# The first layer's MLP up-projection by Strassen's seven block products

## The chip, the cores and the metric

One Trainium2 chip, one core of it. The metric is the device time of one execution in microseconds (us), the median of three runs. Inputs and outputs lie in the chip's memory; all arithmetic is in float32, and each operand of a product is split into a rounded part (hi) and a rest (lo), so that a product of two matrices is three TensorE products: hi x hi, hi x lo, lo x hi.

## The reference

Two layers over 512 latent rows and 256 context rows of width 1024. What matters here is the MLP sub-layer of the first layer, which runs over all 768 rows:

```python
def sq_relu_mlp(h, lw):
    return jnp.square(jax.nn.relu(h @ lw["w1"])) @ lw["w2"]

x = layer_norm(alpha * x + g2 * sq_relu_mlp(modulate(x, sh2, sc2), lw), ln2_g[l], ln2_b[l])
```

w1 is 1024 x 4096 and w2 is 4096 x 1024. The factors sh1, sc1, g1, sh2, sc2, g2 ("modulation vectors") of each layer are six pieces of 1024 of silu(c) @ w_ada + b_ada, one set for the latent stream and one for the context stream.

## The kernel before

The kernel is written with a framework that tracks what each instruction reads and writes, sets the waits and schedules the instructions of each engine ahead of time: an instruction is placed once its operands and its buffer are expected to be free, earlier program text first. On the chip each engine then runs its list in that order.

**The first layer's MLP** (`mlp`, from L1215). The 768 rows stand transposed in two halves of 384 tokens (`hT[0]`, `hT[1]`), hi and lo. The 4096 hidden columns go in eight groups of 512 (NGRP = 8), each in four units of 128 columns. For a group, every unit is multiplied with each half over eight K chunks: 24 products of 128x128 by 128x384, accumulated in one PSUM bank (`termsA`, `chain` at L151). The bank is read by ScalarE (relu, L1236) and VectorE (square, L1237), and the square is split to hi (ScalarE cast, L145) and lo (VectorE subtraction, L146) in `U`. Then the group's down-projection: for each half of the output columns and each of six row tiles, twelve products of 512 columns over the group's four units, added to the row sums `acc` by VectorE (L1276; by ScalarE in group 0). The last group's down-projection is in `mlp_end`, with the layer norm behind it.

**Weights.** w1 comes in loads of 512 KB on SP's queue to the tile `raw` (three buffers, shared with all other loads), and is split to tiles `wh` (ScalarE) and `wl` (VectorE), five buffers each (`unitsA`; L145, L146). w2 likewise (`unitsB`, `split`; L140, L141).

**PSUM.** Four single banks (`bank`) and two tiles of two banks (`two`) for the whole kernel.

**Modulation chunks** (`mod_chunk`, L371 on). 512 columns of a modulation vector set: eight multiply-adds per stream on VectorE (L381, L383) from four loads of 512 KB, a split, two one-row products, an addition (L392), a store. A chunk is six steps; `next(mods)` in other code takes one step, so that the chunks run beside that code. The chunks of layer 1 all run in the first layer's MLP: four of two streams, then eight of one stream. Eight chunks of layer 0 run beside the gate projections of layer 0 (`gates`); beside those of layer 1 none do.

**Other pieces of the stage.** In group 6 the gated residual is taken up (L1279 on GpSimd, L1280 on VectorE) from row tiles loaded ahead. After group 5 the first weights of layer 1 are loaded (`self.early`, `unitsB(..., ahead=True)`).

Of the kernel before, what the change touches and what calls it, by code (L numbers as in the profile page):

```python
# [10 lines left out]
F32 = mybir.dt.float32  # L11
# [22 lines left out]
def shape_tables():  # L34
    """Constants that depend on the shapes alone."""
# [45 lines left out]
    # even and odd frequencies of the latent rows' first half  # L81
# [8 lines left out]
class Act:  # L90
    """transposed rows: per part (hi, lo) the tiles [128, k1 - k0, n] with their ranges of K chunks"""
# [13 lines left out]
class Build:  # L105
    def __init__(self, tc, A):
        self.tc, self.nc, self.A = tc, tc.nc, A
        self.es = ExitStack()
        self.n = 0
        self.nsplit = 0  # L110
        self.om = {}

# [16 lines left out]
    def raw(self, pieces, shape):  # L129
        """pieces: (slice in the raw tile, view in DRAM)"""  # L130
        r = self.t(self.wp, shape, "raw", bufs=3)
        for sl, v in pieces:
            self.nc.sync.dma_start(r[sl], v)
        return r
# [17 lines left out]

    def bank(self):
        return self.t(self.ps, [128, 512], "one", bufs=4)
# [7 lines left out]
    def unitsA(self, view, c0, nchunk, K=8):  # L162
        """units of 128 output columns over all K chunks; two units from two loads of half the K chunks"""
# [10 lines left out]
    def unitsB(self, view, k0, nk, colpieces, scale=None, ahead=False):  # L174
        """per K chunk the (hi, lo) views of the given output columns, times scale; in tiles of their own if ahead"""
# [20 lines left out]

    def termsA(self, unit, act, sl=slice(None), K=8):
# [6 lines left out]
    def termsB(self, lh, units, cols=slice(None)):  # L204
        """lh(k) -> (hi, lo) views [128, 128 tokens]"""
# [6 lines left out]
    def rstd(self, ms, n):  # L212
        """(ms + eps) ** -0.5, in place"""
# [7 lines left out]
    def ln_stats(self, x, st=None):  # L221
        """(mean, rstd) columns of the rows x; st has the halves' statistics if given"""
# [17 lines left out]
    def modulate(self, x, pool, cols, act, sl, quick, sums=None):  # L240
        """layer norm of the rows x, modulated, transposed, to the columns sl of act; a generator of its stages"""
# [5 lines left out]
        else:  # L247
            # the mean from the sums, the squared deviations on the scalar engine
# [19 lines left out]
        if quick:  # L268
            # half the chunks each on the vector and the scalar engine
# [20 lines left out]
    def skew(self, starts, start, newest=False, fill=iter(()), at=0):  # L290
        """a generator for each of the starting stages; within a stage the oldest or the newest first; a step of fill per stage from the given one on"""
# [25 lines left out]
    def mod_start(self, pool):  # L317
        """shift and scale of the first layer's first sub-layer: three quarters on the tensor engine, one on the vector engine; a generator of its pieces"""
# [51 lines left out]
    def mod_chunk(self, l, q, streams, pool):  # L370
        """512 modulation columns: products and sums over K chunks on the vector engine, the sum over partitions by a ones row; a generator of its pieces"""  # L371
# [28 lines left out]
    def load_cols(self, l, sub, s):  # L400
        """scale + 1 and shift as columns"""
# [20 lines left out]
    def where(self, i):  # L422
        """half and columns of token tile i"""
# [14 lines left out]
    def fourier(self, l, pre):  # L438
        """pre: the projected rows, of each token tile or of each column half and two tiles"""
# [3 lines left out]
        with ExitStack() as es:  # L443
# [8 lines left out]
            for t in range(2):  # L452
                # sum and difference of the halves of the latent rows
# [60 lines left out]
    def small_proj(self, l, hT, es_mla, es_gqa):  # L514
# [9 lines left out]
        # four heads by all tokens, or all heads by half the tokens  # L524
# [3 lines left out]
        with ExitStack() as es:  # L528
            tp = self.pool(es, f"sp{l}")
            def rope_tables(nm, scale):  # L530
                """rotary cos and signed sin with the gain folded in"""
# [24 lines left out]
            def normT(n, gain, dst, i):  # L556
                """the rows n [128, 256] transposed, by gain, to dst [128, 2, 2, tokens]"""
# [14 lines left out]
            def rope(pool_tag, kn, nh, cos, sin, i, bufs):  # L572
                """a + b = the rotated kn [128, nh, 64]"""
# [120 lines left out]
    def gates(self, l, hT, tp):  # L694
# [4 lines left out]
        mods = self.mod_chunks(0, [(q, 2) for q in range(4, 12)], tp) if l == 0 else iter(())  # L699
# [510 lines left out]
    def mlp(self, l, hT, pre, rp, lq):  # L1210
# [15 lines left out]
        for g in range(NGRP):  # L1226
# [4 lines left out]
            def w1(j, unit, h, n0, n, ps=None):  # L1231
# [7 lines left out]
                if g:  # L1239
                    next(mods, None)  # L1240
# [301 lines left out]
```

## Time and profile before

| | |
|---|---|
| time, median of 3 runs | 2323.4 us (2322.81 to 2329.74) |
| profiled execution, span from first to last instruction | 2328.0 us |
| TensorE busy | 2251.7 us (97%), mean granted clock 0.988 |
| VectorE busy | 1469.0 us (63%) |
| ScalarE busy | 1006.4 us (43%) |
| GpSimd busy | 341.4 us (15%) |
| mean DMA rate | 123 GB/s |

The profiled execution is one run, on its own; its time beyond the span is not listed, so its span stands for it. It lies 4.6 us above the median of the runs. Busy time is the union of an engine's instructions; the products are pipelined, so the duration of one is longer than the distance to the next, and the pace is read from start to start.

### The profile page before, as it was taken

The numbers are of one execution on the slowest core, as the hardware profiler recorded it, in microseconds if no ns is written. First come the engines' busy times: TensorE is split into PE (matmuls) and PEld (weight loads), VectorE is DVE, ScalarE is ACT, GpSimd is POOL, SyncE is SP. The second block draws the span as 40 slices with busy tenths as digits, with TensorE's granted clock in tenths as the row PEclk, the third lists the DMA queues.
The fourth block names the chain that finished last, engine by engine and source line by source line (L and its number), as shares of the span: only waits on it lengthen the run. The fifth ranks groups of instructions, "written<-read, shape, count | busy, mean of one in ns | idle before, by whom it ended". The sixth has DMA issues, their size and how long they took to land. (4 is left out here: it accounts for less than half of the span.)

```text
span 2328.0 us, 32063 instructions
## 1 busy us (share of the span) xinstructions
PE 2251.7 (97%) x12120; PEld 1975.9 (85%) x12120; DVE 1469.0 (63%) x2389; ACT 1006.4 (43%) x1958; POOL 341.4 (15%) x368
## 2 busy tenths in 40 slices
PE   7999999999999999999999989999999998999997
PEld 3899999888889788888999978888778877888886
DVE  5746567678787774756664574344587886444457
ACT  3433333676664463222232255334566645333321
POOL 1112121111212220000000241222001112000015
PEclk9999999999999999999999999999999999999999
DMA  7444444334238342444453214343133364323322
GB/s 251 130 127 137 146 137 123 104 107 135 71 92 269 130 161 82 137 128 144 136 163 127 66 66 133 105 128 118 64 97 85 100 207 132 100 92 115 120 91 81
DMA packets 243529, 287.44 MB, mean 123 GB/s; under 512 B 51576, under 2 KB 171004, under 8 KB 243376
## 3 DMA queue, kind: packets, MB, share of 16 engines
q1 hardware_dynamic: 229320, 268.02, 36.8%
q10 hardware_dynamic: 14056, 17.39, 2.1%
q8 instruction: 95, 1.56, 0.3%
q14 instruction: 58, 0.48, 0.1%
HBM read 244.40 MB, written 40.96 MB: 123 GB/s over the span
## 5 line engine op out<-in xcount | busy, mean ns | idle before, releaser
L151 PE MATMUL one<-hbA,wh 128*128 128x384 f32 (+2 forms) x2624 | 730.6, 350 | 2.1 <-DVE bg L856 1.0
L151 PEld LDWEIGHTS one<-hbA,wh 128*128 128x128 f32 x2624 | 478.8, 189 | 29.5 <-DVE bg L856 1.3
L151 PE MATMUL one<-hbA,wl 128*128 128x384 f32 (+1 forms) x1168 | 404.4, 346 | 0.3 <-DVE wl L146 0.3
L151 PE MATMUL one<-wh,hbA 128*128 128x256 f32 (+2 forms) x1336 | 303.8, 317 | 5.2 <-ACT hbA L145 3.8
L145 ACT CAST wh<-raw 128x512 fp32r<-128x512 f32 (+1 forms) x233 | 142.3, 636 | 310.6 <-PE one L151 181.0
L146 DVE TENSOR_TENSOR wl<-raw,wh 128x512 fp32r<-128x512 f32 (+1 forms) x233 | 165.5, 731 | 142.4 <-ACT wh L145 141.8
L151 PEld LDWEIGHTS one<-wh,hbA 128*128 128x128 f32 x1336 | 223.1, 190 | 27.9 <-ACT hbA L145 6.5
L151 PEld LDWEIGHTS one<-hbA,wl 128*128 128x128 f32 x1168 | 220.5, 189 | 9.6 <-DVE wl L146 0.8
L141 DVE TENSOR_TENSOR wl<-raw,wh 128x1024 fp32r<-128x1024 f32 (+3 forms) x110 | 137.6, 1252 | 132.4 <-ACT wh L140 131.9
L151 PE MATMUL one<-wl,hbA 128*128 128x256 f32 (+2 forms) x682 | 209.4, 316 | 4.2 <-DVE wl L141 3.3
L151 PE MATMUL one<-wh,u 128*128 128x512 f32 x640 | 199.0, 390 | 0.0
L140 ACT CAST wh<-raw 128x1024 fp32r<-128x1024 f32 (+3 forms) x110 | 112.4, 1023 | 154.7 <-PE one L151 84.8
L383 DVE SCALAR_TENSOR_TENSOR macc<-raw,silu,macc 128x512 f32<-128x512 f32 x224 | 159.5, 747 | 8.4 <-DMA raw<-in_w_ada_dram 7.3
L746 DVE TENSOR_REDUCE nm<-two 128x1 f32<-128x768 f32 x132 | 125.2, 951 | 53.5 <-PE two L151 52.9
L151 PEld LDWEIGHTS one<-wh,u 128*128 128x128 f32 x640 | 120.1, 188 | 26.2 <-ACT u L145 1.2
L151 PEld LDWEIGHTS one<-wl,hbA 128*128 128x128 f32 x682 | 127.3, 190 | 14.7 <-DVE wl L141 4.4
L151 PE MATMUL one<-wh,hbB 128*128 128x512 f32 x444 | 139.4, 391 | 0.0
L1279 POOL TENSOR_TENSOR r<-r,gm 128x1024 f32<-128x1024 f32 x10 | 25.4, 2545 | 758.0 <-DMA raw<-in_w_dram 447.1
L1276 DVE TENSOR_TENSOR r<-r,one 128x512 f32<-128x512 f32 x120 | 81.9, 685 | 84.3 <-PE one L151 84.1
L747 ACT ACTIVATE hbA<-two,nm 128x768 f32<-128x768 f32 x132 | 119.5, 906 | 35.5 <-DVE nm L746 34.2
L151 PE MATMUL one<-wl,u 128*128 128x512 f32 x320 | 124.5, 389 | 0.0
L151 PE MATMUL one<-hbB,wh 128*128 128x512 f32 (+1 forms) x320 | 115.9, 371 | 6.5 <-ACT hbB L287 5.8
(302 smaller groups left out, 4069.3 us busy)
## 6 DMA issues: line engine op xcount, KB each, us to landing
raw<-in_w_dram SPq DMA_DIRECT2D x128, 512.0 KB
raw<-in_w_ada_dram SPq DMA_DIRECT2D x80, 512.0 KB
raw<-in_w_in_dram SPq DMA_DIRECT2D x72, 512.0 KB
gT<-g ACTq DMA_DIRECT2D x48, 192.0 KB
ada<-in_w_ada_dram SPq DMA_DIRECT2D x16, 512.0 KB
raw<-in_w_o_dram SPq DMA_DIRECT2D x16, 512.0 KB
raw<-in_w_fo_dram SPq DMA_DIRECT2D x24, 256.0 KB
bg<-gT SPq DMA_DIRECT2D x32, 192.0 KB
```

Of the source, the lines that this page charges most:

```text
L140: nc.scalar.copy(hi, src)
L141: nc.vector.tensor_sub(lo, src, hi.bitcast(F32))
L145: self.nc.scalar.copy(hi, src)
L146: self.nc.vector.tensor_sub(lo, src, hi.bitcast(F32))
L151: self.nc.tensor.matmul(out, l, r, start=(i == 0), stop=(i == n - 1))
L383: nc.vector.scalar_tensor_tensor(acc[s], r[:, k, :], sc, acc[s], op0=ALU.mult, op1=ALU.add)
L746: nc.vector.tensor_reduce(nm, ps[:, :, :384], axis=AXY, op=ALU.max, negate=True)
L747: nc.scalar.activation(hd["ex"][:, i, :].rearrange("p (a b) -> p a b", a=2), ps[:, :, :384], AF.Exp, bias=nm, scale=1.0, accum_out=rs[:, i ...
L1276: nc.vector.tensor_add(acc[i][:, c], acc[i][:, c], ps)
L1279: nc.gpsimd.tensor_tensor(acc[i], acc[i], gms[i // 4], op=ALU.mult)
```

## The change

The up-projection of groups 1 to 7 of the first layer is done by Strassen's scheme (Winograd's form). The left matrix (two units of 128 hidden columns by two halves of K) and the right matrix (two halves of K by two halves of the tokens) are 2x2 blocks; seven block products of four K chunks give the four blocks of the result in place of eight. `left7` makes the weights' blocks and sums and splits them, from two loads in a ring of their own (`left`, four buffers). `right7` makes the sums of the activations once, in group 0: T1, T2, T4 in tiles of their own, T3 in the place of a block that is used up. `seven` runs the products of a pair in four banks: p1 is copied out of bank a before a second block product is added to it; banks b and c take a second one after VectorE has added their first to p1 or u3. Its first stage is A11; the last stage (S4) is run behind the next pair's first. `psum(8, 0)` gives the stage eight single banks, `psum(4, 2)` restores the earlier division. Of layer 1's modulation chunks only the four of two streams stay in the stage; the eight others go to the gate projections of layer 1, two steps a unit. The residual moves into group 7, the early load of layer 1's weights behind group 7. `U` lies in one pair of buffers for all groups.

```diff
+    def psum(self, ones, twos):
+        if self.ps_es is not None:
+            self.ps_es.close()
+        self.ps_es = ExitStack()
...
+        self.ps = self.pool(self.ps_es, f"ps{self.nps}", space=PSUM)
+        self.ones = ones
+
     def bank(self):
-        return self.t(self.ps, [128, 512], "one", bufs=4)
+        return self.t(self.ps, [128, 512], "one", bufs=self.ones)
...
+    def left7(self, view, c0, pool):
+        nc = self.nc
+        r = [self.t(pool, [128, 4, 256], "left", bufs=4) for _ in range(2)]
+        for q in range(2):
+            nc.sync.dma_start(r[q], view[:, 4 * q:4 * q + 4, c0:c0 + 256])
+        a11, a21 = r[0][:, :, 0:128], r[0][:, :, 128:256]
+        a12, a22 = r[1][:, :, 0:128], r[1][:, :, 128:256]
+        L = {}
+
+        def part(name, src):
+            self.nsplit += 1
+            w = L[name] = self.t(self.wp, [128, 2, 4, 128], "wh" if self.nsplit % 2 else "wl", F32R, bufs=self.NW)
+            self.split_to(w[:, 0], w[:, 1], src)
+
+        comb = lambda dst, x, y, op: nc.vector.tensor_tensor(dst, x, y, op=op)
+        part("A11", a11)
+        part("A22", a22)
+        comb(a22, a21, a22, ALU.add)
+        comb(a21, a11, a21, ALU.subtract)
+        comb(a11, a22, a11, ALU.subtract)
+        part("S2", a11)
+        part("S1", a22)
+        part("S3", a21)
+        part("A12", a12)
+        comb(a12, a12, a11, ALU.subtract)
+        part("S4", a12)
+        return L
+
+    def seven(self, L, R, n, pool, out, last):
...
+        a = self.bank()
+        prod(a, "A11", "B11")
+        p1 = tmp()
+        nc.scalar.copy(p1, a[:, :n])
+        yield
+        b = self.bank()
+        prod(b, "S2", "T2")
+        u2 = tmp()
+        nc.vector.tensor_add(u2, b[:, :n], p1)
+        c = self.bank()
+        prod(c, "S1", "T1")
+
+        def c11():
+            prod(a, "A12", "B21", False)
+            out(0, 0, a[:, :n], True)
+
+        if not last:
+            c11()
+        prod(b, "S3", "T3", False)
+        u3 = tmp()
+        nc.vector.tensor_add(u3, b[:, :n], p1)
+        c22 = tmp()
+        nc.vector.tensor_add(c22, c[:, :n], u3)
+        d = self.bank()
+        prod(d, "A22", "T4")
+        nc.vector.tensor_tensor(u3, u3, d[:, :n], op=ALU.subtract)
+        if last:
+            c11()
+        out(1, 0, u3, False)
+        out(1, 1, c22, False)
+        yield
+        prod(c, "S4", "B22", False)
+        nc.vector.tensor_add(u2, c[:, :n], u2)
+        out(0, 1, u2, False)
+        yield
+
+    def right7(self, act, n, pool):
...
+        def whole(b, k):
+            x = tmp()
+            nc.gpsimd.tensor_tensor(x, b(0, k).bitcast(F32), b(1, k).bitcast(F32), op=ALU.add)
+            return x
...
+        def first():
+            for k in range(4):
+                x12, x11 = whole(act(0, 1), k), whole(R["B11"], k)
+                nc.vector.tensor_tensor(x12, x12, x11, op=ALU.subtract)
+                keep("T1", k, x12)
+                yield
+                x22, x21 = whole(R["B22"], k), whole(R["B21"], k)
+                nc.vector.tensor_tensor(x22, x22, x12, op=ALU.subtract)
+                keep("T2", k, x22)
+                nc.vector.tensor_tensor(x21, x22, x21, op=ALU.subtract)
+                keep("T4", k, x21)
+                yield
...
     def gates(self, l, hT, tp):
...
-        mods = self.mod_chunks(0, [(q, 2) for q in range(4, 12)], tp) if l == 0 else iter(())
+        mods = self.mod_chunks(l, [(q, 2 - l) for q in range(4, 12)], tp)
...
-            next(mods, None)
+            for _ in range(3 - self.NH):
+                next(mods, None)
...
+    def mlp7(self, l, hT, pre, rp):
...
+        mods = self.mod_chunks(1, [(q, 2) for q in range(4)], up)
...
+        def square(U, j, h, x, psum):
+            if psum:
+                a = self.t(up, [128, NB], "sum", bufs=8)
+                nc.scalar.activation(a, x, AF.Relu)
+                nc.vector.scalar_tensor_tensor(a, x, 0.0, a, op0=ALU.max, op1=ALU.mult)
+            else:
+                a = x
+                nc.scalar.activation(a, a, AF.Relu)
+                nc.scalar.activation(a, a, AF.Square)
+            self.split_to(U[h][:, j, 0], U[h][:, j, 1], a)
...
+                Ls = [self.left7(v1, (g * gcf + j) * 128, up) for j in range(0, gcf, 2)]
+                late = None
+                for j, L in zip(range(0, gcf, 2), Ls):
+
+                    def out(f, t, x, psum, j=j):
+                        square(U, j + f, t, x, psum)
+                        next(mods, None)
+
+                    p = self.seven(L, R, NB, up, out, j == gcf - 2)
+                    next(p)
+                    if late:
+                        next(late)
+                    next(p)
+                    late = p
+                    if g == NGRP - 1 and j == 0:
+                        residual()
+                next(late)
...
     def run(self):
...
+            if l:
+                lq = self.pool(er, f"lq{l}", side="right")
+                acc, U, w2t, gcf, gms = self.mlp(l, hT, pre, rp, lq)
+            else:
+                acc, U, w2t, gcf = self.mlp7(l, hT, pre, rp)
+                gms = []
+                self.wx = self.pool(er, "we", side="right")
+                self.early = [self.unitsB(self.w("w_in", 1), 0, 8, [(OFF_F, OFF_F + 256)], ahead=True)]
...
-    nc = bacc.Bacc("TRN2", target_bir_lowering=False, num_devices=1)
+    nc = bacc.Bacc("TRN2", target_bir_lowering=False, num_devices=1, dynamic_dma_scratch_size=1024)
```

The down-projection of groups 1 to 6 is as before, with a step of the chunks after every second row tile; in group 0 the steps of `right7` stand in those places. The rest of the diff takes out comments and the branches of `mlp` that only the first layer used.

## Rows read from the trace of the kernel before

**Rows 1.** The page: its first line, and the granted clock in forty slices.
```profile
span 2328.0 us, 32063 instructions
...
PEclk9999999999999999999999999999999999999999
```

**Rows 2.** Busy time by stretch: us, PE, PEld, DVE, ACT, POOL, clock, DMA share, GB/s.
```profile
846.00:899.50 53.50, 52.97 (x260) 46.41 (x259) 27.00 (x45) 21.11 (x38) 0.00 (x0) 1.00 0.25 81
899.50:966.00 66.50, 65.56 (x329) 57.82 (x329) 51.38 (x82) 17.52 (x30) 0.00 (x0) 1.00 0.46 140
966.00:1033.00 67.00, 67.00 (x341) 60.50 (x341) 49.15 (x78) 19.32 (x34) 0.00 (x0) 1.00 0.52 155
...
1233.00:1299.00 66.00, 66.00 (x338) 60.35 (x337) 28.87 (x41) 16.50 (x28) 4.79 (x2) 1.00 0.28 98
1299.00:1333.00 34.00, 34.00 (x192) 33.26 (x191) 21.57 (x26) 10.95 (x19) 10.30 (x4) 1.00 0.27 81
```

**Rows 3.** TensorE's waits from 840 to 1420 us: total us, times, longest.
```profile
PE one L151 <- DVE wl L141: 1.4, 2, 0.8
```

**Rows 4.** Timeline of TensorE: start us, us; up-projection of group 1, down-projection of group 0.
```profile
904.88 0.51 PE L151 MATMUL one<-hbA,wh 128*128 128x384 f32 x2
...
905.40 0.51 PE L151 MATMUL one<-hbA,wh 128*128 128x384 f32 x2
...
884.33 0.39 PE L151 MATMUL one<-wl,u 128*128 128x512 f32 x1
...
885.01 0.39 PE L151 MATMUL one<-wl,u 128*128 128x512 f32 x1
```

**Rows 5.** Groups of instructions by line and shape, 846 to 1345 us.
```profile
L383 DVE SCALAR_TENSOR_TENSOR macc<-raw,silu,macc 128x512 f32<-128x512 f32 x112 | 81.6, 747 | 3.9 <-DMA raw<-in_w_ada_dram 2.8
...
L1276 DVE TENSOR_TENSOR r<-r,one 128x512 f32<-128x512 f32 x72 | 49.0, 684 | 43.1 <-PE one L151 42.9
L141 DVE TENSOR_TENSOR wl<-raw,wh 128x1024 fp32r<-128x1024 f32 x32 | 41.4, 1293 | 32.5 <-ACT wh L140 32.1 <-PE one L151 0.4
L146 DVE TENSOR_TENSOR wl<-raw,wh 128x512 fp32r<-128x512 f32 x56 | 38.4, 711 | 31.8 <-ACT wh L145 31.8
...
L1237 DVE SCALAR_TENSOR_TENSOR relu<-one,relu 128x384 f32<-128x384 f32 x64 | 35.1, 551 | 21.7 <-ACT relu L1236 21.7
...
L145 ACT CAST wh<-raw 128x512 fp32r<-128x512 f32 x56 | 32.8, 619 | 105.0 <-PE one L151 54.2 <-DMA raw<-in_w_dram 50.6
L1236 ACT ACTIVATE relu<-one 128x384 f32<-128x384 f32 x64 | 31.2, 489 | 101.7 <-PE one L151 101.0 <-DVE u L146 0.6
...
L146 DVE TENSOR_TENSOR hbB<-relu,hbB 128x384 fp32r<-128x384 f32 x32 | 17.8, 556 | 9.3 <-ACT hbB L145 9.3
...
L141 DVE TENSOR_TENSOR wl<-macc,wh 128x512 fp32r<-128x512 f32 x16 | 11.0, 688 | 13.4 <-ACT wh L140 13.1
L392 DVE TENSOR_TENSOR macc<-one,raw 1x512 f32<-1x512 f32 x16 | 10.6, 674 | 12.4 <-PE one L151 12.4
...
L381 DVE TENSOR_SCALAR macc<-raw,silu 128x512 f32<-128x512 f32 x16 | 7.5, 482 | 3.5 <-DMA raw<-in_w_ada_dram 1.9 <-DMA md<-macc 1.6
```

**Rows 6.** GpSimd's subtractions of line 833: duration ns min/median/max.
```profile
L833 POOL TENSOR_TENSOR wl<-raw,wl x25: 1272/1290/2006, 428.7 to 1870.9; 128x512 fp32r<-128x512 f32 x25
```

**Rows 7.** Timelines of VectorE and GpSimd at the residual of group 6.
```profile
1313.49 3.42 DVE L141 TENSOR_TENSOR wl<-raw,wh 128x1024 fp32r<-128x1024 f32 x1
...
1320.05 1.22 DVE L141 TENSOR_TENSOR wl<-raw,wh 128x1024 fp32r<-128x1024 f32 x1 [0.40 <-PE one L151]
...
1313.10 2.73 POOL L1279 TENSOR_TENSOR r<-r,gm 128x1024 f32<-128x1024 f32 x1 [1.99 <-issue]
```

**Rows 8.** Timeline of VectorE in group 1: a run of chunk steps.
```profile
905.20 2.73 DVE L383 SCALAR_TENSOR_TENSOR macc<-raw,silu,macc 128x512 f32<-128x512 f32 x4
```

**Rows 9.** Busy time by stretch, the projections of layer 0 and of layer 1.
```profile
140.00:400.00 260.00, 253.61 (x1650) 246.71 (x1649) 166.00 (x322) 91.74 (x218) 57.01 (x98) 1.00 0.47 141
1430.00:1640.00 210.00, 203.13 (x1158) 178.91 (x1157) 82.48 (x176) 80.66 (x194) 44.28 (x90) 0.98 0.37 113
```

More of the change, by code (lines that the diff above doesn't have):

```diff
@@ new lines, in seven, with prod @@
+    def seven(self, L, R, n, pool, out, last):
+        nc = self.nc
+        def prod(ps, l, r, first=True):
+            w = L[l]
+            ts = []
+            for k in range(4):
+                h, o = R[r](0, k), R[r](1, k)
+                ts += [(w[:, 0, k], h), (w[:, 0, k], o), (w[:, 1, k], h)]
+            for i, (x, y) in enumerate(ts):
+                nc.tensor.matmul(ps[:, :n], x, y, start=(first and i == 0), stop=(i == 11), skip_group_check=not first)
+        tmp = lambda: self.t(pool, [128, n], "sum", bufs=8)
+        a = self.bank()
[31 more added lines that the diff above has]
+        yield
@@ new lines, in right7, with keep, second @@
+    def right7(self, act, n, pool):
+        nc = self.nc
+        T = {x: self.t(pool, [128, 2, 4, n], x, F32R, bufs=1) for x in ("T1", "T2", "T4")}
+        tmp = lambda: self.t(pool, [128, n], "sum", bufs=8)
+        R = {"B11": act(0, 0), "B21": act(1, 0), "B22": act(1, 1), "T3": act(0, 1)}
+        for x in T:
+            R[x] = lambda p, k, t=T[x]: t[:, p, k]
+        def whole(b, k):
+            x = tmp()
+            nc.gpsimd.tensor_tensor(x, b(0, k).bitcast(F32), b(1, k).bitcast(F32), op=ALU.add)
+            return x
+        def keep(name, k, x):
+            self.split_to(R[name](0, k), R[name](1, k), x)
+        def first():
+            for k in range(4):
+                x12, x11 = whole(act(0, 1), k), whole(R["B11"], k)
[8 more added lines that the diff above has]
+                yield
+        def second():
+            for k in range(4):
+                x22, x12 = whole(R["B22"], k), whole(act(0, 1), k)
+                nc.vector.tensor_tensor(x22, x22, x12, op=ALU.subtract)
+                keep("T3", k, x22)
+                yield
+        return R, first(), second()
@@ L1217, in mlp @@
         up = self.pool(es, f"u{l}")
-        mods = self.mod_chunks(1, [(q, 2 if q < 4 else 1) for q in range(12)], up) if l == 0 else iter(())
         gms = []
@@ L1229, in mlp @@
             else:
-                U = [self.block([128, gcf, 2, NB], small=(l == 0)) for _ in range(self.NH)]
+                U = [self.block([128, gcf, 2, NB]) for _ in range(self.NH)]
             def w1(j, unit, h, n0, n, ps=None):
@@ L1238, in w1 @@
                 self.split_to(U[h][:, j, 0, n0:n0 + n], U[h][:, j, 1, n0:n0 + n], a[:, :n])
-                if g:
-                    next(mods, None)
             if g == 0:
                 us = self.early
-                for h, n0, n in [(h, 0, NB) for h in range(2)] if self.NH == 2 else [(0, 0, 256), (0, 256, 256)]:
+                for h, n0, n in [(0, 0, 256), (0, 256, 256)]:
                     for j, unit in enumerate(us):
@@ L1260, in mlp @@
                 n = NT // self.NH
-                x1 = [self.block([128, n, D], F32, small=(l == 0)) for _ in range(self.NH)]
+                x1 = [self.block([128, n, D], F32) for _ in range(self.NH)]
                 for i in range(NT):
```

89 lines of the change are left out of this document (72 added, 17 removed).

## The prediction

> **What bounds the kernel now.** I read the page first: the span is 2328.0 us and TensorE's granted clock stands in the top tenth of its scale in all forty slices [rows 1]. Then the table of stretches over the first layer's MLP, cut at its groups [rows 2]: from 966 us to 1333 us TensorE is busy in the whole of each stretch, at a granted clock of 1.00, which is its level of 2.4 GHz; the stretch from 899.5 us loses 0.94 us and the group before it 0.5 us. In the list of TensorE's waits from 840 us to 1420 us the largest on VectorE is 1.4 us [rows 3]. So this stage is paid product by product: work taken from TensorE shortens the run, and a wait put on it lengthens the run, one for one. VectorE is busy 51.4 us of 66.5 us in group 1 and 49.2 us of 67 us in group 2, but 28.9 us of 66 us in group 6 [rows 2]; the difference is the modulation chunks that the first groups carry.
>
> **What is removed.** The timeline of group 1 gives the pace: the same place in the pattern of three products of 384 columns comes round from 904.88 us to 905.40 us, so 0.52 us for three or 0.173 us each [rows 4]. In the down-projection three products of 512 columns take 884.33 us to 885.01 us, 0.68 us or 0.227 us each [rows 4]. Check: a group has 192 products of 384 and 144 of 512 columns, 33.3 us + 32.6 us = 65.9 us, and the stretches are 66 us to 67 us. Two up-projection units cost 2 units x 2 halves x 8 K chunks x 3 = 96 products before; seven block products of 4 K chunks x 3 are 84. Twelve fewer in each of 14 pairs (two in each of groups 1 to 7) are 168 fewer, x 0.173 us = **29.1 us**. A group becomes 168 x 0.173 us + 32.6 us = 61.7 us, of which the up-projection is 29.1 us.
>
> **VectorE and ScalarE in a group.** Prices are the means of [rows 5]. Per pair VectorE now has 7 splits and 4 weight sums of 128x512 (11 x 0.711 us = 7.8 us; the sums have no row, their nearest is the subtraction of the same strided shape), and per pair five sums of accumulators, one square and four splits of 128x384 (10 x 0.555 us = 5.6 us). Two pairs, four splits of w2 (1.293 us) and 12 additions to the rows (0.684 us) make 26.8 + 5.2 + 8.2 = 40.2 us of 61.7 us. ScalarE has per pair 7 x 0.619 us and 12 passes of about 0.5 us, 20.7 us for two pairs beside 29.1 us of products. Without the chunks this hides.
>
> With the chunks of groups 1 and 2 it does not quite. Group 1 shows 51.4 us now; group 6 without its two residual steps of 1.2 us shows 26.5 us, so the chunks take some 24.9 us. 40.2 + 24.9 = 65.1 us against 61.7 us: 3.4 us a group, **6.8 us** for two. Bounds: nothing if the chunks slip into group 3, where some 21 us of VectorE are free; at the top, if they go strictly in program order, the up-projection of group 1 carries eight of the 24 chunk steps. A chunk is 14 x 0.747 us, two starts, two splits and two last additions, with about 0.5, 0.69 and 0.674 us each [rows 5], 14.2 us or 2.4 us a step; eight are 18.9 us. Beside 11.1 us of accumulators, 9.2 us of second-pair weights and 2.6 us of w2 that is 41.8 us in 29.1 us: 12.7 us a group, 25.4 us for two. I take 6.8 us since [rows 2] show the chunks spread today.
>
> **Tables of summed activations.** In group 0 GpSimd makes 24 sums of 128x384. None is in the trace; 1.29 us for 128x512 [rows 6] scales to 0.97 us, 23.3 us in all, VectorE adds 32 steps x 0.556 us = 17.8 us, beside 53.5 us in which VectorE is busy 27.0 us [rows 2]. They fit if they overlap: 0 us. If they take turns: 17.8 + 23.3 us, 4.4 us of u splits, 5.2 us of w2 and 6.4 us of group 1's first weights are 57.1 us, 3.6 us too many. The row for turns is plain: a VectorE subtraction that began at 1313.49 us, while a GpSimd product ran from 1313.10 us for 2.73 us, took 3.42 us, and its like at 1320.05 us took 1.22 us [rows 7]. Nearer to the second end, I take **2 us**. The Trainium skill's page "SBUF — State Buffer", section "Who interferes with whom", says that a VectorE instruction with two SBUF inputs and a GpSimd one that reads SBUF exclude each other for the whole instruction; the trace agrees by that 3.42 us against 1.22 us. By that rule this term is 3.6 us, not 2 us.
>
> **Waits inside a pair.** Three times a pair TensorE comes back to a bank that VectorE or ScalarE must first have read (A12 after the copy of p1, S3 after u2, S4 after c22). A product is 12 x 0.173 us = 2.1 us. Mostly two products lie between, 4.2 us; before S3 of the second pair only one, 2.1 us, against a read of 0.55 us. So a read may queue some 3.6 us, there 1.5 us. What it queues behind is a run of chunk steps: four took 2.73 us at 905.20 us [rows 8]. Cost nothing without chunks; the cost with them is the 6.8 us above.
>
> **The turn to the down-projection.** Its third K chunk needs the square of C11, whose last product ends one product (2.1 us) and six of 512 columns (1.4 us) earlier, 3.4 us. Relu, square, cast and subtraction are four steps of about 0.53 us [rows 5], 2.1 us. One run of four chunk steps ahead costs 1.4 us; none, nothing. I take 0.36 us x 7 = **2.5 us**, between 0 and 9.8 us.
>
> **What moves.** Eight single-stream chunks go to layer 1's projections: 8 x (7 x 0.747 + 0.5 + 0.69 + 0.67) = 56.7 us on VectorE and 32 loads of 512 KB on SP's queue and the three staging buffers. VectorE there is busy 82.5 us of 210 us; with them 139 us, 66%. Layer 0's same loops, with twice the streams, run at 166 us of 260 us, 64%, and TensorE is busy in 253.6 us of the 260 us against 203.1 us of 210 us in layer 1 [rows 9]. So the cover exists; bounds are nothing and the 6.4 us that layer 0 lacks, I take **0.5 us**. Their 16 products of 512 columns (3.6 us) leave the MLP and come back here: no sum. The residual (eight loads, six GpSimd products) moves past group 6 on SP and POOL, and the next layer's first two loads go behind it, ahead of the last four of w2: 14 loads through three buffers. At the 140 GB/s of group 1 [rows 2] a load takes 3.7 us and 14 take 52 us, against 16.3 us of group 6's second half plus 29.1 us: 7 us late at worst. Rates vary (155 GB/s in group 2), so between 0 and 7 us I take **1 us**.
>
> **The sum.** -29.1 + 6.8 + 2 + 2.5 + 0.5 + 1 = -16.3 us. The profiled execution has a span of 2328.0 us and would have 2311.7 us; it lies 4.6 us over the median of the three runs (2323.4 us), so the median becomes **2307 us**.
>
> **Rivals.**
> *All covered.* Chunks slip into group 3 and every read comes in time: 2323.4 - 29.1 = 2294 us; up to 7 us of waits still counts as this case. For it: VectorE at 65% without chunks; against: [rows 8]. Chance 0.25.
> *Turns in group 0.* If the first chunk (14.2 us), which runs in this stretch today, also stands ahead of the tables, group 1 starts 3.6 us to 17.8 us late instead of 2 us: 2309 us to 2323 us, middle 2316 us. For it: [rows 7]; against: the tables come first in program order. Chance 0.10, of which 0.07 still faster by over 0.3%. The Trainium skill's rule above is this mechanism.
> *VectorE becomes the bound.* The chunks hold program order in groups 1 and 2: 25.4 us instead of 6.8 us, 2326 us, no change. For it: the code calls one step per output. Against: today they run elsewhere. Chance 0.13.
> *Re-entry waits, the slower side.* If reads queue q us on average in all 14 pairs, 35 re-entries lose q - 3.6 and the 7 short ones q - 1.5. At q = 4.1 us that is 36 us, and from there the kernel is slower; at 4.5 us it is 53 us, 2323.4 + 24 = 2347 us. For it: runs of 2.73 us exist, and a ScalarE queue holding weight casts would delay p1 too. Against: groups 3 to 7 have no chunks. Chance 0.07.
>
> **How the numbers follow.** The forecast has 0.45 (2301 us to 2314 us). Faster by over 0.3% (7 us, about what a measurement of this kernel can tell): 0.45 + 0.25 + 0.07 = 0.77; within: 0.13 + 0.03 = 0.16; slower: 0.07. The range 2294 us to 2325 us takes in the covered case, the turns and the better half of the bound case, and leaves out its worse half and the slow one.
>
> **What would show it.** Right: 168 fewer products of 384 columns; groups 3 to 6 at about 62 us with TensorE busy throughout; VectorE near full in groups 1 and 2 and TensorE waiting there some 7 us on it. Wrong: groups 3 to 6 longer than 64 us (re-entry or the turn), more than 4 us before group 1's second block product (tables), new TensorE waits in layer 1's projections over 3 us, or the last group's down-projection waiting on a load.

## The result, and the profile after

The changed kernel takes 2347.23 us (median of 4 runs, 2345.69 to 2350.12) against 2325.39 us for the kernel before (4 runs, 2322.81 to 2329.74): ratio 1.0091, interval 1.0077 to 1.0106. It is 21.8 us slower; 2307 us was forecast. The profiled execution's page, first line and TensorE's busy time:

```profile
span 2345.1 us, 32008 instructions
...
PE 2232.3 (95%) x11952; PEld 1951.8 (83%) x11952; DVE 1572.8 (67%) x2547; ACT 1062.1 (45%) x2072; POOL 374.4 (16%) x392
```

TensorE has 168 products fewer than before (12120), as forecast. The stretches of the first layer's MLP, cut about at groups 1 to 6 and the last up-projection (columns as in [rows 2]):

```profile
893.00:976.00 83.00, 70.81 (x328) 61.66 (x327) 68.66 (x109) 32.40 (x58) 0.00 (x0) 0.92 0.36 108
976.00:1048.00 72.00, 65.25 (x320) 57.37 (x319) 56.73 (x94) 25.53 (x47) 0.00 (x0) 0.95 0.38 118
1049.00:1110.00 61.00, 61.00 (x310) 55.42 (x309) 36.04 (x58) 23.02 (x42) 0.00 (x0) 1.00 0.22 69
...
1234.00:1296.00 62.00, 62.00 (x314) 56.31 (x314) 38.76 (x60) 23.35 (x42) 7.18 (x3) 1.00 0.24 77
1296.00:1336.00 40.00, 31.35 (x169) 31.03 (x168) 28.38 (x37) 15.68 (x29) 7.90 (x3) 0.87 0.33 109
```

From first product to first product, groups 3 to 6 take 61.8 us each (forecast: 61.7), TensorE full at clock 1.00. Group 1 takes 81.6 us (894.55 to 976.18), group 2 72.4 us, the last up-projection 40.2 us in place of 29.1 us, and in these three the granted clock is 0.92, 0.95 and 0.87. TensorE's waits from 840 us to 1420 us, where [rows 3] had 1.4 us as VectorE's largest, then group 1's first products and the five places of the waits in TensorE's timeline (the rows left out belong to the layer norms ahead of the MLP and behind it):

```profile
PE one L247 <- DVE sum L258: 15.6, 2, 8.6
PE one L152 <- ACT wh L141: 7.0, 2, 5.0
...
PE one L152 <- DVE wl L142: 4.7, 1, 4.7
```

```profile
894.55 2.27 PE L247 MATMUL one<-hbA,wh 128*128 128x384 f32 x12
...
897.38 2.00 PE L247 MATMUL one<-T,wh 128*128 128x384 f32 x10 [0.21 <-DVE wh L147]
...
910.85 4.17 PE L247 MATMUL one<-hbA,wh 128*128 128x384 f32 x12 [6.93 <-DVE sum L258]
939.68 2.93 PE L152 MATMUL one<-wh,hbB 128*128 128x512 f32 x6 [4.97 <-ACT wh L141]
1008.52 1.21 PE L152 MATMUL one<-wh,hbB 128*128 128x512 f32 x4 [2.05 <-ACT wh L141]
1014.43 0.80 PE L152 MATMUL one<-wl,hbB 128*128 128x512 f32 x1 [4.70 <-DVE wl L142]
1313.04 4.21 PE L247 MATMUL one<-hbA,wh 128*128 128x384 f32 x12 [8.65 <-DVE sum L258]
```

Three causes stand in these rows: VectorE's u2 (L258) late in group 1, w2's weights late in groups 1 and 2, u2 late again in group 7. Together they are 27.3 us. Behind the long waits come slower products: twelve of 384 columns take 4.17 us and 4.21 us, against 2.27 us at 894.55 us. The granted clock while they run is 0.50, TensorE's lower level (1.2 GHz). Group 1 above 61.8 us is 19.8 us: 11.9 us of these waits, 1.8 us of chunk products, and some 6 us that I put down to slower products; the like sum for group 2 and the last up-projection leaves 2 us and 2.4 us. So some 38 us are lost in an MLP that had 29.1 us to win and 3.6 us of chunk products to hand on.

From group 1's first product to layer 1's Fourier step the changed kernel takes 512.8 us (894.55 us to 1407.39 us), the kernel before 508.9 us (898.63 us to 1407.51 us): the whole gain is used up, and 4.0 us more. The rest of the loss is behind it. From the Fourier step to the same late score product of layer 1's first head (1644.88 us before, 1663.02 us after) TensorE spends 255.6 us in place of 237.4 us, 18.2 us more. That stretch, before and after:

```profile
1408.00:1645.00 237.00, 227.57 (x1317) 201.10 (x1318) 100.53 (x206) 94.98 (x222) 47.72 (x94) 0.99 0.39 122
```

```profile
1407.00:1663.00 256.00, 236.66 (x1340) 205.44 (x1338) 155.02 (x290) 101.44 (x234) 52.20 (x93) 0.97 0.57 175
```

VectorE gained 54 us of work there, as forecast (56.7), and DMA went from 122 to 175 GB/s. TensorE's waits grew: on the softmax's tiles from 3.6 us to 7.3 us, on the rotated key from 2.1 us to 5.3 us; the clock fell from 0.99 to 0.97.

### The profile page after: what moved, and what is told of

The parts are those of the page before. It is cut to its first block, busy times and chain, and to the rows that moved or that the text cites. A ratio compares the mean times of both kernels' runs of the same rounds, so it can differ in the third digit from the quotient of the medians.

```text
span 2345.1 us, 32008 instructions
## 1 busy us (share of the span) xinstructions
PE 2232.3 (95%) x11952; PEld 1951.8 (83%) x11952; DVE 1572.8 (67%) x2547; ACT 1062.1 (45%) x2072; POOL 374.4 (16%) x392
## 5 line engine op out<-in xcount | busy, mean ns | idle before, releaser
L152 PE MATMUL one<-hbA,wh 128*128 128x384 f32 (+2 forms) x1728 | 502.7, 358 | 1.5 <-DVE g L1209 0.5
L152 PEld LDWEIGHTS one<-hbA,wh 128*128 128x128 f32 x1728 | 316.4, 190 | 27.2 <-DVE g L1209 0.9
L152 PE MATMUL one<-wh,hbB 128*128 128x512 f32 x828 | 262.2, 395 | 7.1 <-ACT wh L141 7.0
L152 PE MATMUL one<-hbA,wl 128*128 128x384 f32 (+1 forms) x720 | 254.0, 353 | 0.0
L152 PEld LDWEIGHTS one<-wh,hbB 128*128 128x128 f32 x828 | 157.8, 191 | 41.3 <-ACT wh L141 7.7
L511 DVE SCALAR_TENSOR_TENSOR macc<-raw,silu,macc 128x512 f32<-128x512 f32 x224 | 159.6, 747 | 12.7 <-DMA raw<-in_w_ada_dram 11.4
L152 PE MATMUL one<-wl,hbB 128*128 128x512 f32 x414 | 162.8, 394 | 4.7 <-DVE wl L142 4.7
L152 PEld LDWEIGHTS one<-hbA,wl 128*128 128x128 f32 x720 | 136.3, 189 | 9.0 <-DVE wl L147 0.2
L876 ACT ACTIVATE hbA<-two,nm 128x768 f32<-128x768 f32 x132 | 119.5, 905 | 40.2 <-DVE nm L875 38.8
L899 PE MATMUL one<-ident,hbA 128*128 128x128 f32 x768 | 115.4, 274 | 0.8 <-ACT hbA L876 0.6
L152 PE MATMUL one<-hbB,wl 128*128 128x512 f32 (+1 forms) x304 | 111.9, 368 | 0.0
L899 PEld LDWEIGHTS one<-ident,hbA 128*128 128x128 f32 x768 | 93.8, 141 | 17.7 <-issue 1.5
```

Source lines behind the costliest of these rows:

```text
L152: self.nc.tensor.matmul(out, l, r, start=(i == 0), stop=(i == n - 1))
L511: nc.vector.scalar_tensor_tensor(acc[s], r[:, k, :], sc, acc[s], op0=ALU.mult, op1=ALU.add)
L876: nc.scalar.activation(hd["ex"][:, i, :].rearrange("p (a b) -> p a b", a=2), ps[:, :, :384], AF.Exp, bias=nm, scale=1.0, accum_out=rs[:, i ...
L899: nc.tensor.transpose(pt[:, i * 128:(i + 1) * 128], hd["ex"][:, i, tt * 128:(tt + 1) * 128], self.ident)
```

## The experiments

The kernel before was measured again beside each set of runs; its medians went from 2324.57 us to 2326.34 us, and by so much a difference between kernels of two sets can be off. "Kernel 10" is the kernel of experiment 10.

**1. The moved chunks alone**, put into the kernel before.

```diff
-        mods = self.mod_chunks(0, [(q, 2) for q in range(4, 12)], tp) if l == 0 else iter(())
+        mods = self.mod_chunks(l, [(q, 2 - l) for q in range(4, 12)], tp)
...
-            next(mods, None)
+            for _ in range(3 - self.NH):
+                next(mods, None)
...
-        mods = self.mod_chunks(1, [(q, 2 if q < 4 else 1) for q in range(12)], up) if l == 0 else iter(())
+        mods = self.mod_chunks(1, [(q, 2) for q in range(4)], up) if l == 0 else iter(())
```

> The kernel before, with nothing of the change but the move of layer 1's eight single-stream modulation chunks from the first layer's MLP to the gate projections of layer 1. Theory (the move is a cost of its own): the stretch from layer 1's first position-transform product to its first score products, 236.6 us before and 255.6 us after the change, grows to 252 to 257 us, the first layer's MLP gets 3.6 us shorter, and the time is 2336 to 2342 us, 11 to 17 us over before. Rival (the projections only suffer under the new layout and order that the block products bring): the stretch stays under 245 us and the time within 5 us of before.

Measured: 2341.23 us against 2326.34 us, ratio 1.0065 (1.0041 to 1.0089): **+14.9 us** for a part that I had at 0.5 us. The stretch in layer 1 is 255.1 us, as in the changed kernel, 17.7 us more than before. From group 1's first product to the Fourier step it takes 505.0 us in place of 508.9 us, about the 3.6 us of the chunks' products; 17.7 us less these 3.9 us is 13.8 us, so the cost lies in layer 1.

**2. The moved loads, most of their arithmetic left out** (kernel of experiment 1).

```diff
-                        nc.vector.scalar_tensor_tensor(acc[s], r[:, k, :], sc, acc[s], op0=ALU.mult, op1=ALU.add)
+                        n = 512 if l == 0 or streams == 2 else 1
+                        nc.vector.scalar_tensor_tensor(acc[s][:, :n], r[:, k, :n], sc, acc[s][:, :n], op0=ALU.mult, op1=ALU.add)
```

> The kernel before with the eight single-stream chunks moved to layer 1's projections, as in the run that moved them whole, but there seven of the eight multiply-adds of each chunk work on one column instead of 512: the loads, the splits and the chunk's products stay, most of VectorE's 54 us is gone. It leaves out that arithmetic of layer 1's later shifts, scales and gates. Theory: the move costs 15 us because VectorE, busy 154 of 256 us there with it, comes late with what the next chain needs: without its time the waits on the softmax's and the key's tiles go, and the time is 2320 to 2328. Rival, the loads: they stand in SyncE's queue and in the three staging buffers ahead of the projections' own weights: then it stays at 2336 to 2341.

Measured: 2336.18 us, ratio 1.0044 (1.0029 to 1.0059). The rival's number came, and the theory has a part in it: of the 17.7 us by which experiment 1 lengthens the stretch, 6.4 us go with VectorE's work (248.7 us). 3.6 us are the chunks' own products. What is left, some 8 us, stays with the loads and with the chunks' remaining steps; these two were not told apart, and the cause of this part stays open.

**3. No chunk at all in the first layer's MLP.** Layer 1's first four chunks are left out; its first shifts and scales are read from layer 0's.

```diff
+        if l == 1 and sub == 0:
+            m, o = self.mods[0][s], 3 * D
...
-        mods = self.mod_chunks(1, [(q, 2) for q in range(4)], up)
+        mods = iter(())
```

> The changed kernel with layer 1's first four modulation chunks left out (layer 1's first shift and scale are then read from another place, so its numbers are others). Theory (chunk steps on VectorE and chunk loads on SP's queue make groups 1 and 2 late): group 1 falls from 81.6 us and group 2 from 72.4 us to 62 to 64 us each, group 7's up-projection stays at about 40 us against 29.1 us, the time is 2312 to 2320 us. Rival (GpSimd's sums in group 0 hold VectorE up and so make group 1 late): the wait of 6.9 us before S3 of the first pair stays above 5 us, group 1 stays above 70 us, the time is 2325 to 2335 us.

Measured: 2322.59 us, ratio 0.9988 (0.9976 to 1.0001), 2.6 us over the theory's range. Group 1 falls to 63.2 us with one wait of 1.10 us, group 2 to 61.8 us; group 7 keeps its 8.65 us. So the waits of groups 1 and 2 need the chunks, and group 7's is another matter.

**4. The sums for the tables on VectorE.** In the changed kernel GpSimd makes them, in the stretch from 800 us to 893 us (columns as in [rows 5]):

```profile
L147 DVE TENSOR_TENSOR T<-sum,T 128x384 fp32r<-128x384 f32 x12 | 12.1, 1025 | 0.0
...
L297 POOL TENSOR_TENSOR sum<-hbA,hbA 128x384 f32<-128x384 f32 x24 | 30.0, 1265 | 17.1 <-DVE hbB L147 5.9 <-DVE hbA L416 3.1 <-DVE sum L306 3.0
```

A sum takes 1.265 us where I had 0.97 us, and VectorE's subtraction beside it 1.025 us where [rows 5] have 0.556 us. So VectorE enters group 1 late: it ends the tables 2.2 us before that group's first product. Its timeline:

```profile
898.45 7.37 DVE L511 SCALAR_TENSOR_TENSOR macc<-raw,silu,macc 128x512 f32<-128x512 f32 x11
...
910.25 0.55 DVE L258 TENSOR_TENSOR sum<-one,sum 128x384 f32<-128x384 f32 x1
```

S2's products ended at about 899.3 us; the sum that frees their bank ran 11 us later, behind eleven multiply-adds of chunks and the second pair's weights. The edit:

```diff
-            nc.gpsimd.tensor_tensor(x, b(0, k).bitcast(F32), b(1, k).bitcast(F32), op=ALU.add)
+            nc.vector.tensor_tensor(x, b(0, k).bitcast(F32), b(1, k).bitcast(F32), op=ALU.add)
```

> The changed kernel with the 24 sums of activations on VectorE instead of GpSimd, so that the two engines take no turns in group 0. Theory (chunks): VectorE has 24 x 0.55 us more in group 0 and still the chunks; group 1 stays between 76 and 84 us and the time within 5 us of the changed kernel, 2342 to 2352 us. Rival (turns): VectorE's table subtractions fall from 1.03 us to 0.56 us, the wait before S3 of group 1's first pair falls under 2 us, group 1 falls under 73 us and the time to 2336 to 2340 us.

Measured: 2340.17 us, ratio 1.0053 (1.0035 to 1.0071), 7.1 us under the changed kernel. The sums and the subtractions now take the same time and less than half of GpSimd's:

```profile
L297 DVE TENSOR_TENSOR sum<-hbA,hbA 128x384 f32<-128x384 f32 x24 | 12.5, 548 | 0.0
...
L147 DVE TENSOR_TENSOR T<-sum,T 128x384 fp32r<-128x384 f32 x12 | 6.5, 549 | 0.0
```

The 6.93 us become 0.87 us and group 1 takes 71.6 us. The waits on w2 stay: 5.00 us in group 1, 2.11 and 3.90 us in group 2. The edit moved more than the sums, since the framework laid VectorE's list out anew: the tables end 6.1 us before group 1's first product, 4.0 us earlier than in the changed kernel, and between them and u2 stand nine multiply-adds of chunks in place of thirteen. So u2 comes 7.0 us earlier, and the turns alone are not all of it.

**5. The residual's gate products on VectorE.** Group 7 of the changed kernel, VectorE first, then GpSimd:

```profile
1298.67 1.23 DVE L1376 SCALAR_TENSOR_TENSOR r<-raw,r 128x1024 f32<-128x1024 f32 x1 [2.51 <-POOL r L1375]
...
1301.01 2.88 DVE L147 TENSOR_TENSOR wh<-left,wh 128x512 fp32r<-128x512 f32 x1
...
1305.02 3.35 DVE L1376 SCALAR_TENSOR_TENSOR r<-raw,r 128x1024 f32<-128x1024 f32 x1
...
1308.90 1.21 DVE L1376 SCALAR_TENSOR_TENSOR r<-raw,r 128x1024 f32<-128x1024 f32 x1
...
1312.44 0.54 DVE L258 TENSOR_TENSOR sum<-one,sum 128x384 f32<-128x384 f32 x1
```

```profile
1300.57 2.78 POOL L1375 TENSOR_TENSOR r<-r,raw 128x1024 f32<-128x1024 f32 x1 [1.94 <-DVE r L1427]
1304.57 2.72 POOL L1375 TENSOR_TENSOR r<-r,raw 128x1024 f32<-128x1024 f32 x1 [1.22 <-DVE r L1427]
```

The turn that [rows 7] showed in group 6, where TensorE lost nothing by it: a 0.68 us subtraction takes 2.88 us and a 1.21 us step 3.35 us, each beside a GpSimd product. That is 4.3 us. Ahead of it VectorE stands idle four times, at 1283 to 1299 us, for 2.5 us each until a GpSimd product is there (the first line is the last of them). u2 comes behind all of it.

```diff
-                nc.gpsimd.tensor_tensor(acc[i], acc[i], gm[s], op=ALU.mult)
+                nc.vector.tensor_tensor(acc[i], acc[i], gm[s], op=ALU.mult)
```

> The changed kernel with the six gate products of the residual on VectorE instead of GpSimd. Theory (in group 7 VectorE stands behind GpSimd's products, 3.35 us and 2.88 us for steps of 1.2 us and 1.3 us): the wait of 8.6 us before S3 of the first pair falls under 4 us although VectorE has six steps of 1.2 us more, group 7's up-projection falls from 40.2 us to 30 to 36 us, the time is 2337 to 2343 us. Rival (the weights' sums queue late for another reason): the wait stays above 7 us, the time within 4 us of the changed kernel.

Measured: 2341.81 us, ratio 1.0062 (1.004 to 1.0084), 5.4 us less. The 8.65 us are gone, the last up-projection takes 29.2 us; a wait of 1.69 us on w2 comes in their place.

**6. The chunk's store on GpSimd's queue**, in all stages that have chunks.

```diff
-            nc.sync.dma_start(self.mods[l][s][q * 512:(q + 1) * 512].unsqueeze(0), r)
+            nc.gpsimd.dma_start(self.mods[l][s][q * 512:(q + 1) * 512].unsqueeze(0), r)
```

> The changed kernel, with one edit: the store of a finished chunk goes from GpSimd's queue instead of SyncE's. Theory: in the first group that has the seven products, the two loads of the down-projection's weights stand on SyncE's queue right behind the chunk's store, which waits for VectorE's last addition of the chunk; that is the 4.97 us wait of TensorE at 939.68 us. With the store on a queue that carries nothing else, those loads go out some 5 us earlier: that wait falls under 1 us, and with the half-speed products behind it (about 2 us) the time falls by 4 to 8 us, to 2339 to 2343. Rival, the staging buffers: the loads wait for a buffer that the chunk's arithmetic on VectorE gives back; then the wait stays at 4 us or more and the time within 2 us of 2347.

Measured: 2361.43 us, ratio 1.0151 (1.0134 to 1.0169): 14 us slower than the changed kernel, and the waits on w2 stay (4.67 and 1.81 us, 4.08 and 3.03 us). The theory fell. In this run VectorE's timeline (the two last additions of a chunk) and SP's queue show the rival's place:

```profile
935.53 0.67 DVE L520 TENSOR_TENSOR macc<-one,raw 1x512 f32<-1x512 f32 x1
...
936.67 0.67 DVE L520 TENSOR_TENSOR macc<-one,raw 1x512 f32<-1x512 f32 x1
```

```profile
902.45 0.25 SPq L134 DMA_DIRECT2D raw<-in_b_ada_dram  x1
905.10 3.02 SPq L134 DMA_DIRECT2D raw<-in_w_ada_dram  x2
...
937.37 5.75 SPq L134 DMA_DIRECT2D raw<-in_w_dram  x2
```

Three staging buffers: the bias row takes one at 902.45 us, the next chunk's loads the two others, and w2's first load goes out at 937.37 us, as the second addition that reads the bias row ends. That addition follows the chunk's products, which stand ahead of the last block product of the up-projection in TensorE's list. In group 2 it is not the bias row: in the changed kernel the loads of w2 go out at 1003.85 us and 1009.69 us, held 2.6 us and 5.4 us by multiply-adds of chunks (L511) that give their buffers back. Of the 14 us about 7 are there at the MLP's end, 2 of them as group 1 begins, and 6 more come in layer 1's stretch (262.0 us), where GpSimd has work of its own; why so much was not pursued.

**7. The three edits 4, 5 and 6 together** (their diffs, nothing else).

> The changed kernel with three edits at once: the 24 sums for the tables on VectorE, the residual's gate products on VectorE, the chunk's store on GpSimd's queue. Theory: the three waits are separate, so the savings add: 7.1 us and 5.4 us as measured alone, and 4 to 8 us for the store: 2327 to 2331, level with the kernel before, the seven groups at 65, 66, 62, 62, 62, 62 us and the last up-projection at 30 us; what then still stands against the kernel before is the 15 us of the chunks moved to layer 1's projections. Rival: VectorE has no room in the first two such groups, and a wait that goes comes back at the next product that needs VectorE: above 2334.

Measured: 2341.56 us, ratio 1.0063 (1.0047 to 1.008). The savings did not add: the waits on w2 were still 14.3 us, and edit 6 costs in layer 1 (261.2 us).

**8. Kernel 7 with the eight chunks back in the first layer's MLP.**

```diff
-        mods = self.mod_chunks(l, [(q, 2 - l) for q in range(4, 12)], tp)
+        mods = self.mod_chunks(0, [(q, 2) for q in range(4, 12)], tp) if l == 0 else iter(())
...
-        mods = self.mod_chunks(1, [(q, 2) for q in range(4)], up)
+        mods = self.mod_chunks(1, [(q, 2 if q < 4 else 1) for q in range(12)], up)
...
-            if g == NGRP - 3:
+            if g == NGRP - 2:
```

> The kernel of the run before it (three edits), with the eight single-stream chunks back in the first layer's MLP, their steps going on through the groups 3 to 6, whose VectorE is busy 37 of 62 us. Theory: the 54 us of chunk arithmetic on VectorE fit there (about 13 to 18 us in each group), their 16 products cost 3.6 us wherever they stand, and layer 1's projections fall from 255 us back to about 237: 2310 to 2316. Rival, the order on VectorE: a chunk step put between an eviction and the product that needs it holds TensorE up in each of these groups by 2 us or more, with half-speed products behind each wait: 2318 to 2328.

Measured: 2334.6 us, ratio 1.0037 (1.0027 to 1.0048). That is over both forecasts. Layer 1's stretch is back at 236.7 us; the waits on w2 go on, some 18.7 us in groups 1, 2, 4 and 5 and 1.2 us in the last group.

**9. Own buffers for the chunks in the MLP**, in the changed kernel: the bias row in a tile of its own, the chunk's weights in the left factors' ring, the store on GpSimd's queue, all in this stage alone.

```diff
+            if own:
+                r = self.t(pool, [128, 2, 512], "left", bufs=4)
+                nc.sync.dma_start(r, view[:, 2 * g:2 * g + 2, q * 512:(q + 1) * 512])
...
+        if own:
+            b = self.t(pool, [1, 512], "bias", bufs=1)
+            nc.sync.dma_start(b, A["b_ada"][l, q * 512:(q + 1) * 512].unsqueeze(0))
...
+            (nc.gpsimd if own else nc.sync).dma_start(self.mods[l][s][q * 512:(q + 1) * 512].unsqueeze(0), r)
```

> The changed kernel with that same edit alone (chunk weights in the left factors' buffers, bias row in a tile of its own, store from GpSimd's queue, in the first layer's MLP only). Theory: of the changed kernel's waits in the MLP the three on the down-projection's weights go (4.97, 2.05 and 4.70 us, 11.7 together, with 2 to 3 us of half-speed products behind them); the 6.93 and 8.65 us on VectorE's sum stay: 2332 to 2338. Rival: VectorE's order holds the group up anyway, and the time stays at 2341 or more.

Measured: 2344.65 us, ratio 1.0078 (1.0056 to 1.0099). All waits on w2 are gone, as expected (which of the edit's three parts did it was not told apart), yet the rival's time came: the wait at group 1's S3 grew from 6.93 to 16.18 us. VectorE's list and what TensorE waited for:

```profile
898.47 0.88 DVE L513 TENSOR_SCALAR macc<-left,silu 128x512 f32<-128x512 f32 x2 [3.73 <-DMA left<-in_w_ada_dram]
...
904.40 2.74 DVE L515 SCALAR_TENSOR_TENSOR macc<-left,silu,macc 128x512 f32<-128x512 f32 x4 [3.73 <-DMA left<-in_w_ada_dram]
```

```profile
917.12 4.03 PE L247 MATMUL one<-hbA,wh 128*128 128x384 f32 x12 [16.18 <-DVE sum L258]
```

The chunk steps still stand ahead of the sum, and now wait for loads whose buffers a late VectorE gives back late.

**10. Edits 4, 5, 8 and 9 together.**

> The run with three edits and the chunks back in the first layer's MLP, with one more edit there: a chunk's weights load into the four buffers of the left factors, its bias row into a tile of its own, its result leaves from GpSimd's queue (the layers' projections keep the old places), so that the three staging buffers carry the down-projection's weights alone. Theory, from the traces: the bias row sat in one of those three buffers until VectorE's addition behind the chunk's products, at the very end of a group's up-projection, and the first load of the down-projection's weights had to take that very buffer; TensorE's waits on those weights were 20 us over five groups (15.1 on the rounded, 4.9 on the residual parts). They go to under 4 us, and with the half-speed products behind them the time falls from 2335 to 2304 to 2312, under the kernel before. Rival: the left factors of the next group now wait for VectorE's chunk steps to give their buffers back, and the wait moves to the first products of each group: 2320 or more.

Measured: **2297.83 us** (2294.99 to 2301.31) against 2324.74 us, ratio 0.9874 (0.9848 to 0.9900): 26.9 us faster than the kernel before, and 6 us under the theory's range. Three stretches (columns as in [rows 2]):

```profile
1376.00:1613.00 237.00, 227.01 (x1319) 200.26 (x1320) 101.27 (x206) 95.76 (x224) 48.43 (x94) 0.99 0.40 123
893.00:976.00 83.00, 81.42 (x416) 73.24 (x415) 79.12 (x130) 33.40 (x61) 2.22 (x4) 1.00 0.47 141
976.00:1049.00 73.00, 73.00 (x373) 65.55 (x372) 66.98 (x111) 30.21 (x56) 2.42 (x5) 1.00 0.48 143
```

The first is layer 1's stretch, 237.0 us as before. In the second VectorE is busy 79 of 83 us and TensorE loses 1.6 us, at clock 1.00: a nearly full VectorE was no bound once its order fitted.

**11. Kernel 10 with the chunks in layer 1 again** (edit 8 undone).

> The run of 2297.8 us with one thing undone: the eight single-stream chunks stand in layer 1's projections again, as the change has them. Theory: their move costs there what it cost the kernel before, 15 us, since nothing of it depends on the first layer's MLP: 2311 to 2316. Rival: in the kernel before the move also freed that MLP (its end came 8 us earlier), and here it frees it too, whose groups 3 to 6 are full on TensorE either way; then the price is what the projections alone grew by, 18 to 19 us: 2316 to 2319.

Measured: 2310.26 us, ratio 0.994 (0.9924 to 0.9957). The move costs 12.4 us (14.9 us in experiment 1). Layer 1's stretch grows by 18.6 us (255.6 us) and its Fourier step starts 6.7 us earlier, at 1369.18 us, 2.0 us of them ahead already as group 1 begins. This kernel is the changed one with three placements mended (the sums, the residual's products, the chunks' buffers): 37.0 us less, and a Fourier step 38.2 us earlier, 36.0 us if counted from group 1's first product. That is about what the five waits and the slower products came to. Its groups 1 and 2, and the time behind them:

```profile
892.00:1050.00 158.00, 156.50 (x803) 141.62 (x802) 140.32 (x229) 67.86 (x123) 4.16 (x8) 1.00 0.42 130
1050.00:1300.00 250.00, 250.00 (x1264) 227.17 (x1263) 160.70 (x248) 93.90 (x171) 0.00 (x0) 1.00 0.23 74
```

**12. Kernel 10 with the sums on GpSimd again** (edit 4 undone).

> The run of 2297.8 us with one thing undone: the 24 sums for the tables run on GpSimd again, as the change has them, while VectorE takes the differences. Theory: sums and differences take turns, VectorE enters the first group that has seven products some 9 us late with the chunk steps still ahead of the sum that the third product needs, and TensorE waits there 7 to 16 us, then runs slower for some us: 2308 to 2320. Rival, no cost once the loads are in time: the chunk steps that were behind late loads were the delay, not the turns: 2296 to 2302.

Measured: 2316.05 us, ratio 0.9967 (0.9957 to 0.9978): the sums on GpSimd cost 18.2 us here.

```profile
915.80 4.21 PE L247 MATMUL one<-hbA,wh 128*128 128x384 f32 x12 [15.91 <-DVE sum L258]
```

One wait of 15.91 us; from 893 us to 950 us the granted clock is 0.85. As in experiment 4 the list is another one too. The tables end 2.4 us before group 1's first product, in kernel 10 7.3 us before it; between them and u2 stand eleven multiply-adds of chunks in place of four, and VectorE is idle 9.8 us there, waiting for the chunks' loads, in place of 0.9 us. So the 18.2 us are the price of where the sums stand; how much of it is the turns, and how much the list, no run separates.

## Why the prediction was wrong

Its sign was wrong: 21.8 us slower in place of 16.3 us faster. Four terms of the sum carry that: the tables, the chunks, the residual and layer 1's projections. The -29.1 us that are removed, 37.0 us for three of them together (experiment 11) and 14.9 us for the move (experiment 1) make +22.8 us.

- **What is removed, 29.1 us: right.** 168 products fewer, 61.8 us a group where nothing else interferes, an up-projection of some 29 us in experiment 5.
- **The tables, 2 us (0 to 3.6 us): the step that failed first.** The mechanism was named, its price was not found. I asked when the tables would be finished; they were in time (TensorE waits 0.21 us in group 1's second block product, on a weight). I did not ask what VectorE had in its list behind them: thirteen multiply-adds of chunks and the second pair's weights, all ahead of u2. With the sums on VectorE the time falls by 7.1 us in the changed kernel and by 18.2 us in kernel 10, the turns and the other list together. GpSimd's 24 sums took 30.0 us, not the 23.3 us scaled from [rows 6]. The Trainium skill's rule of turns ("SBUF — State Buffer", "Who interferes with whom"), by which such a VectorE instruction and a GpSimd one that reads SBUF exclude each other, is borne out by 1.025 us against 0.549 us for the same subtraction. The rival of turns had a part of the cause and too small a price.
- **Waits inside a pair: the step "what it queues behind is a run of chunk steps" was right, the length wrong.** It took four steps, 2.73 us, from [rows 8], a VectorE that was on time; eleven stood there, 7.37 us.
- **Chunks in groups 1 and 2, 6.8 us (0 to 25.4 us): in the range, for another reason.** I costed VectorE's time. That is worth 1.5 us (experiment 11: TensorE 156.5 of 158 us). What cost 11.7 us of waits was how w2's loads share staging buffers and SP's queue with the chunks: in group 1 the bias row, whose buffer comes free near the end of the up-projection, in group 2 the chunks' weights, whose buffers come free with VectorE's multiply-adds. With own buffers all of it went (experiment 9). The prediction followed the loads of w2 in group 7 only.
- **The residual, 1 us (0 to 7 us).** I counted its loads. Its GpSimd products delay VectorE's steps ahead of u2, by turns (4.3 us) and by four waits of 2.5 us for their results: 8.65 us of wait, 5.4 us of it to be had back alone. [rows 7] showed that turn; I used it for group 0 only, and did not look for the waits.
- **Layer 1's projections, 0.5 us (0 to 6.4 us): mis-sized beyond its range**, 12.4 to 14.9 us. VectorE is at 155 of 256 us, not far from the share I compared with, but layer 0's stretch in [rows 9] is not a cover for layer 1's: about a third of the growth is VectorE's arithmetic, a fifth the products, the rest stays even without most of the arithmetic, and what causes it is open.
- **The turn to the down-projection, 2.5 us: nothing.** TensorE is full from 1050 us to 1300 us (experiment 11).
- **Missing: the clock.** The sum had waits at their length alone. About 10 us more went in slower products behind them.

The rival on the slower side gave 2347 us, the very time measured, and was wrong all the same: it wanted 4.5 us of queue in all 14 pairs, and two pairs waited. A number that fits does not make a mechanism. The three placements are worth 37.0 us and the move 12.4 us; with both mended the seven products give 2297.8 us, near the 2294 us of the case "all covered", whose cover had to be made.

## What to carry to other kernels

Where each engine runs a list made ahead, cost a slowed engine by what stands next in its list, not by its spare time, and look there for filler work ahead of something that TensorE needs. An edit that moves work to another engine can also reorder that list, so compare the lists before the gain is put down to the engine. Follow each load to the instruction that gives its buffer back: a bias row of 512 numbers held up the weights of group 1's down-projection. Work that hid well in one stage has to be shown hidden in the next by that stage's own waits.

## What the runs showed of the hardware that was not expected

- A TensorE wait is dearer than its length. Behind 6.93, 8.65 and 16.18 us the next twelve products took 4.17, 4.21 and 4.03 us in place of 2.27 us, and the stretch from 893 us to 950 us in experiment 12 ran at a granted clock of 0.85.
- GpSimd is slow at what VectorE does fast: a 128x384 sum 1.265 us against 0.548 us, and beside it VectorE's instruction on two SBUF operands can take about as long (1.37 us at 877.18 us in the changed kernel, against 0.55 us). Moving 24 sums to the busier engine shortened the run.
- Small stores moved from SP's queue to GpSimd's cost 14 us where every stage used it (experiment 6), for a reason that is open. Experiments 9 to 12 use it in the first layer's MLP alone, and no wait of TensorE on a store shows there.
